# An RWKV and band-attention encoder layer: the sample streams' eight RWKV steps as a second chain beside the prompt's first sixteen

## The chip, the cores and the metric

One core of one Trainium2 chip. The time is the device time of one execution in microseconds (us), the median of several runs. Lower is better.

## What is computed

One inference step of a one-layer streaming encoder, in float32, with d_model 1024, 1024 prompt rows of one new stream and 16 rows of each of 8 running sample streams:

```python
x = x + 0.5 * SwiGLU_1(RMSNorm(x))
P = RMSNorm(x) @ w_in        # r,k,v + three loras for RWKV-7; q,k,v for attention
mix = concat(RWKV7(P_rwkv), BandAttn(P_att)) @ w_out
x = x + mix
x = x + 0.5 * SwiGLU_2(RMSNorm(x))
y = RMSNorm_final(x)

def step(s, inp):            # RWKV-7, per head: state s is 64 x 64, one row after the other
    sa = einsum('bhvk,bhk->bhv', s, kk_t)
    s = s * w_t - sa * (kk_t * a_t) + v_t * k_t
    y_t = einsum('bhvk,bhk->bhv', s, r_t)
```

The prompt begins with a zero state, each sample stream with one from the inputs (`state_wkv`), and every last state is an output. Eight heads of 64 in either group. Attention looks back over a band of eight chunks of 64.

## The kernel before, in words

The kernel runs through stages: the first feed-forward block, the projection `P` with the preparation of the RWKV factors, the projection of attention's values, the RWKV chain beside attention, the output projection, the second feed-forward block. The rows are cut into 9 tiles of 128, eight of the prompt and one of the samples. Products are made of split high and low parts of the operands, three matmuls for one.

**The RWKV chain.** Rows are taken 32 at a time (`L`): 32 prompt steps that follow one another, since each takes the state that the one before left, and 8 steps of the sample streams (one per stream, 16 rows), which take a state from the inputs and have nothing to do with each other. They are grouped by four: groups i = 0 to 7 are the prompt, 8 and 9 the streams. One step (in `_rwkv_run`, L942) is a chain from engine to engine: eight small matmuls into `ps_c` (L961, called pw below), a copy `wx` on VectorE (L963), eight matmuls (L966, pu), four copies into `mov` in turn on VectorE and ScalarE (L969), eight matmuls that make the next state (L971, wst), and two multiplications on VectorE (L984) that write the state into the next step's `mov`. Beside it eight matmuls into `ps_yc` (L975) and a copy of ScalarE (L986) give the step's output. A group's output is normalized a step at a time during the next group (`_rwkv_post`, L1014: VectorE, GpSimd, ScalarE, four transposes into `ps_y` on TensorE at L1038, and four multiplications `yo` at L1042). States come in by `_sample_states` (L929: load `sin`, four transposes into `ps_si`, a copy) and go out by `_state_out` (L1000: transposes into `ps_so`, a copy `so`, a store from SP's queue). `ps_yc`, `ps_si`, `ps_so` and `ps_y` are all one PSUM bank (`_post_bank`, L925), and `ps_c` is another.

**The order of the work.** The tile scheduler gives every engine one fixed list of instructions. It follows the order of the program, and an instruction that waits holds those behind it on its engine. The program (L1389 to L1424) writes 12 prompt steps, then `_attention_inputs` (L545), whose 432 matmuls into `ps_av` (L567 to L569) need nothing of the chain and stand between its steps on TensorE. After them the program has one group of the chain, then six units of attention, and so on. `_attention` (L1203) has 72 units (a pair of heads, a row tile, a head of the pair), 18 to each of four pairs of heads. Its loads (`q`, `kt`, `v`, `bias`) are issued on GpSimd's queue, the RWKV loads on SP's.

Of the kernel before, what the change touches and what calls it, by code (L numbers as in the profile page):

```python
# [9 lines left out]
F32 = mybir.dt.float32  # L10
# [6 lines left out]
P = 128  # L17
# [9 lines left out]
HD = 64  # L27
# [850 lines left out]
def _chunk_constants(k, a):  # L878
    nc = k.nc

    def t(shape, name):
        return k.rw.tile(shape, F32, tag=name, bufs=1, name=name)


    k.wst = [t([P, NPAIR, 2, 2, P], f"wst{i}") for i in range(2)]
    for w in k.wst:
        nc.vector.tensor_copy(w[0:HD].rearrange("r p e i (h d) -> r (p e i h) d", d=HD),
                              k.ident[0:HD, None, 0:HD].to_broadcast([HD, 4 * NH, HD]))


def _rwkv_load(k, i):
# [7 lines left out]
    rw = k.rw  # L899
# [3 lines left out]
    if j == 0:  # L903
        k.tt = rw.tile([P, 2, 8, L], F32, tag="tt", bufs=2, name="tt")
        nc.sync.dma_start(k.tt.rearrange("s a c t -> s (a c t)"), k.inv[:, :, g].rearrange("b s x t -> (b s) (x t)"))
    q.tt = k.tt[:, :, cj]
# [15 lines left out]
    return q  # L922
# [19 lines left out]
def _rwkv_run(k, a, i, pq, q, nq):  # L942

    nc = k.nc
    mm = nc.tensor.matmul
    rw = k.rw
    q.y = rw.tile([P, 4, 2, HD], F32, tag="y", bufs=2, name="y")
    post = iter(()) if pq is None else _rwkv_post(k, i - 1, pq)
    fin = None
    if i == 7:  # L950
        fin = rw.tile([HD, 1, NH, HD], F32, tag="y", bufs=2, name="fin")
    for c in range(4):
        cc = 4 * i + c
        mov, wout = q.mov[:, c], q.wout[:, :, c]
        wst = q.wst[:, :, c % 2, c // 2].rearrange("r p (h d) -> r p h d", d=HD)
        pw, pu = (k.cbank[:, 128 * j:128 * j + 128].rearrange("p (a d) -> p a d", a=2)
                  for j in (cc % 2, 1 - cc % 2))
        px = k.cbank[:, 256:].rearrange("p (a d) -> p a d", a=NPAIR)
        for hh in HEAD_ORDER:
            s = slice(L * (hh // 2), L * (hh // 2) + L)  # L960
            mm(pw[s, hh % 2], wout[0:HD + L, hh, 0:L], mov[0:HD + L, hh], start=True, stop=True)  # L961
        wx = rw.tile([P, 2, HD], F32, tag="wx", bufs=2, name="wx")
        nc.vector.tensor_copy(wx, pw)  # L963
        for hh in HEAD_ORDER:
            s = slice(L * (hh // 2), L * (hh // 2) + L)
            mm(pu[s, hh % 2], q.tt[s, hh % 2, c], wx[s, hh % 2], start=True, stop=True)  # L966
        for j in range(4):
            copy = nc.scalar.copy if j % 2 else nc.vector.tensor_copy
            copy(mov[HD + L:P, 2 * j:2 * j + 2], pu[L * j:L * j + L])  # L969
        for hh in range(NH):  # L970
            mm(px[HEADS[hh % 2], hh // 2], wst[:, hh // 2, hh % 2], mov[:, hh], start=True, stop=True)  # L971
        py = _post_bank(k, "ps_yc")[:, :P].rearrange("p (a d) -> p a d", a=2)
        for hh in HEAD_ORDER:
            s = slice(L * (hh // 2), L * (hh // 2) + L)
            mm(py[s, hh % 2], wout[:, hh, L:], mov[:, hh], start=True, stop=True)  # L975
        if i == 7 and c == 3:
            nxt = fin[:, 0]
        elif i >= 8:
            nxt = mov[0:HD]
        else:  # L980
            nxt = q.mov[0:HD, c + 1] if c < 3 else nq.mov[0:HD, 0]
        for h in range(2):
            s = HEADS[h]
            nc.vector.tensor_tensor(nxt[:, h:NH:2], px[s],  # L984
                                    k.pc[s, :, cc:cc + 1].to_broadcast([HD, NPAIR, HD]), ALU.mult)
        nc.scalar.copy(q.y[:, c], py)  # L986
        next(post, None)
        if c == 1 and 7 <= i < 2 * NG - 1:
            _sample_states(k, a, i - 7, nq.mov)
    if i == 2 * NG - 1:  # L990
        for _ in _rwkv_post(k, i, q):
            pass
    if i == 7:
        _state_out(k, fin, lambda p: k.o["wkv_p"][0, 0:1, 2 * p:2 * p + 2])
    elif i >= 8:
        b0 = 4 * (i - 8)
        _state_out(k, q.mov, lambda p: k.o["wkv_s"][0, b0:b0 + 4, 2 * p:2 * p + 2])
# [51 lines left out]


def _rwkv(k, a):
    _chunk_constants(k, a)
    k.cbank = k.psc.tile([P, 512], F32, tag="c", bufs=1, name="ps_c")
    n = 2 * NG
    pq, q = None, _rwkv_load(k, 0)
# [470 lines left out]
```

## Time and profile before

| | |
|---|---|
| median of 3 runs | 2610.01 us (2602.8 to 2616.19) |
| profiled execution, its own time | 2605.25 us |
| its span in the profile | 2603.5 us |
| TensorE busy in the span | 2422.6 us (93%) |
| VectorE, ScalarE, GpSimd busy | 1124.8, 899.8, 1076.5 us |
| value projection ends, first attention softmax, last attention output | 1367.9, 1405.0, 1660.5 us |

Times inside the kernel are read on the profiled execution from the start of its span. The granted clock is the share of full speed that TensorE got in a stretch: 1.00 is 2.4 GHz, 0.50 is 1.2 GHz, and a value between is a mixture of the two. PEld are TensorE's weight loads, and SPq, ACTq are the DMA issues of a queue's engine.

### The profile page before, as it was taken

The page shows a single profiled execution, that of the slowest core. Times are in us where ns is not written, and L with a number is a line of the kernel's source. Part 1 is how long each engine was busy: PE and PEld are TensorE (multiplying, and loading weights), DVE is VectorE, ACT ScalarE, POOL GpSimd, SP SyncE. Part 2 cuts the span into 40 slices and gives each one's busy share as a digit, 9 for nine tenths or more (in the row PEclk, how much of TensorE's full clock was granted, in tenths as well). Part 3 has the DMA queues.
Part 4 walks back from the last instruction along what each step waited for, and adds up shares of the span by engine and source line. Part 5 has one row for each costly group of instructions (what it writes and reads, how often), then busy time and mean ns, then how long its engine had stood idle before and what let it go on. Part 6 is the DMA issues. An engine that isn't in the chain of part 4 may idle for free.

```text
span 2603.5 us, 43481 instructions
## 1 busy us (share of the span) xinstructions
PE 2422.6 (93%) x17415; PEld 2161.5 (83%) x17415; DVE 1124.8 (43%) x2346; ACT 899.8 (35%) x1903; POOL 1076.5 (41%) x966
## 2 busy tenths in 40 slices
PE   4999999988999999999997999897999999989998
PEld 3899999986888799899874666676999999988886
DVE  6322222214544533856854666346222222225555
ACT  5333333321111443443323576524333333321112
POOL 4545454444433233443213443105554544544332
PEclk8999999999999999999996899998999999999999
DMA  3222112227322324543658994522221122252221
GB/s 113 67 68 86 56 63 86 67 83 269 113 77 70 107 63 133 168 132 104 190 148 197 219 206 112 175 91 65 67 86 57 62 86 68 69 197 102 77 102 73
DMA packets 230283, 284.75 MB, mean 109 GB/s; under 512 B 54920, under 2 KB 183552, under 8 KB 227264
## 3 DMA queue, kind: packets, MB, share of 16 engines
q1 hardware_dynamic: 194044, 226.72, 27.8%
q0 software_dynamic: 7648, 25.43, 4.1%
q10 hardware_dynamic: 28388, 29.81, 3.5%
q8 instruction: 137, 2.24, 0.4%
q14 instruction: 66, 0.54, 0.1%
HBM read 191.79 MB, written 90.12 MB: 108 GB/s over the span
## 4 chain that ended last, share of the span: by engine, by line
PE 42%; DVE 5%; POOL 3%; issue 3%; ACT 2%; DMA 2%; ACTq 0%; POOLq 0%; DVEq 0%
PE pa L341 3%; PE pd L450 3%; PE pd L451 3%; PE pd L449 3%; PE pa L343 3%; PE pa L342 3%; PE pb L341 2%; PE pb L342 2%; PE pb L343 2%; POOL frm L292 2%; PE ps_s L1132 1%; PE ps_o L1186 1%; PE ps_pt L1171 1%; PE ps_yc L975 1%; PE ps_wo L1261 1%
## 5 line engine op out<-in xcount | busy, mean ns | idle before, releaser
L341 PE MATMUL pa<-F,frm 128*128 128x256 f32 (+1 forms) x1408 | 424.6, 302 | 34.7 <-ACT r L348 25.2
L343 PE MATMUL pa<-F,frm 128*128 128x256 f32 (+1 forms) x1408 | 419.3, 298 | 2.7 <-POOL frm L292 2.7
L342 PE MATMUL pa<-F,frm 128*128 128x256 f32 (+1 forms) x1408 | 419.3, 298 | 2.1 <-POOL F L272 2.1
L453 DVE TENSOR_TENSOR x<-pd,x 128x512 f32<-128x512 f32 x396 | 270.0, 690 | 243.1 <-PE pd L451 228.8
L163 POOL TENSOR_TENSOR spl<-raw,spl 128x1024 fp32r<-128x1024 f32 x78 | 187.6, 2408 | 453.0 <-ACT spl L162 453.0
L449 PE MATMUL pd<-spl,h 128*128 128x512 f32 x792 | 314.0, 397 | 14.8 <-ACT spl L162 12.1
L450 PE MATMUL pd<-spl,h 128*128 128x512 f32 x792 | 311.9, 394 | 13.3 <-POOL spl L163 13.3
L292 POOL TENSOR_TENSOR frm<-cmb,frm 128x512 fp32r<-128x512 f32 x176 | 230.1, 1309 | 221.7 <-ACT frm L291 221.3
L343 PE MATMUL pb<-F,frm 128*128 128x320 f32 (+1 forms) x1056 | 312.7, 296 | 3.1 <-POOL frm L292 3.1
L342 PE MATMUL pb<-F,frm 128*128 128x320 f32 (+1 forms) x1056 | 312.2, 296 | 3.1 <-DVE F L271 3.1
L341 PE MATMUL pb<-F,frm 128*128 128x320 f32 (+1 forms) x1056 | 313.3, 297 | 1.2 <-ACT frm L291 1.2
L451 PE MATMUL pd<-spl,h 128*128 128x512 f32 x792 | 311.8, 394 | 0.0
L341 PEld LDWEIGHTS pa<-F,frm 128*128 128x128 f32 x1408 | 268.9, 191 | 44.4 <-ACT r L348 33.0
L343 PEld LDWEIGHTS pa<-F,frm 128*128 128x128 f32 x1408 | 269.1, 191 | 3.5 <-POOL frm L292 3.5
L342 PEld LDWEIGHTS pa<-F,frm 128*128 128x128 f32 x1408 | 269.4, 191 | 2.5 <-POOL F L272 2.5
L292 POOL TENSOR_TENSOR frm<-raw,frm 128x512 fp32r<-128x512 f32 x132 | 173.8, 1318 | 186.7 <-ACT frm L291 186.7
L162 ACT ACTIVATE spl<-raw 128x1024 fp32r<-128x1024 f32 x78 | 82.2, 1055 | 406.3 <-PE pd L451 342.7
L343 PEld LDWEIGHTS pb<-F,frm 128*128 128x128 f32 x1056 | 200.2, 190 | 3.8 <-POOL frm L292 3.8
L342 PEld LDWEIGHTS pb<-F,frm 128*128 128x128 f32 x1056 | 200.1, 190 | 3.3 <-DVE F L271 3.3
L341 PEld LDWEIGHTS pb<-F,frm 128*128 128x128 f32 x1056 | 200.0, 189 | 1.8 <-ACT frm L291 1.8
L449 PEld LDWEIGHTS pd<-spl,h 128*128 128x128 f32 x792 | 150.1, 190 | 48.5 <-ACT spl L162 12.3
L450 PEld LDWEIGHTS pd<-spl,h 128*128 128x128 f32 x792 | 150.1, 189 | 48.3 <-POOL spl L163 16.2
(259 smaller groups left out, 4572.7 us busy)
## 6 DMA issues: line engine op xcount, KB each, us to landing
raw<-in_w_ff_gate_dram SPq DMA_DIRECT2D x22, 1024.0 KB
raw<-in_w_ff_up_dram SPq DMA_DIRECT2D x22, 1024.0 KB
raw<-in_w_ff_down_dram SPq DMA_DIRECT2D x44, 512.0 KB
raw<-in_w_in_dram SPq DMA_DIRECT2D x26, 512.0 KB
hr<-hd SPq DMA_DIRECT2D x11, 1152.0 KB
hr<-he SPq DMA_DIRECT2D x11, 1152.0 KB
q<-qk POOLq DMA_DIRECT2D x24, 384.0 KB, 7.6
x<-xd SPq DMA_DIRECT2D x18, 512.0 KB
```

What stands on the lines that cost most here:

```text
L162: k.nc.scalar.activation(dst[:, 0], raw, AF.Copy)
L163: k.nc.gpsimd.tensor_tensor(dst[:, 1], raw, dst[:, 0].bitcast(F32), ALU.subtract)
L292: nc.gpsimd.tensor_tensor(d[:, 1], x, d[:, 0].bitcast(F32), ALU.subtract)
L341: nc.tensor.matmul(ps, frm[:, 0, c], F[:, 0, jj, c], start=new and c == 0, stop=False, **kw)
L342: nc.tensor.matmul(ps, frm[:, 0, c], F[:, 1, jj, c], start=False, stop=False, **kw)
L343: nc.tensor.matmul(ps, frm[:, 1, c], F[:, 0, jj, c], start=False, stop=c == 3, **kw)
L449: mm(ps, h[:, 0, f, a], d[f][:, 0, b], start=f == 0, stop=False)
L450: mm(ps, h[:, 0, f, a], d[f][:, 1, b], start=False, stop=False)
L451: mm(ps, h[:, 1, f, a], d[f][:, 0, b], start=False, stop=f == 1)
L453: nc.vector.tensor_tensor(xs, ps, xs, ALU.add)
L975: mm(py[s, hh % 2], wout[:, hh, L:], mov[:, hh], start=True, stop=True)
L1132: mm(ps, q.qs[i // 3][:, j, h, t:t + P], q.ks[h][:, c0:c0 + n], start=j == 0, stop=j == 1)
```

## The change

The chain is split. `_rwkv` is the prompt alone and yields after every step. `_rwkv_samples` is a second generator for groups 8 and 9, with a pool of its own (`rw2`, one buffer for each of `mov`, `wout`, `wst`, `tt` and `y`) and a PSUM bank of its own (`ps_cs`). Both issue the same step, now `_chunk`. The program writes sixteen prompt steps with a stream step after every second one from the fourth on, then the value projection, then the other sixteen prompt steps with two units of attention after each. To make room, `sin` and `so` share a tag of two buffers (before: four and two), the normalization's square shares the tag of `yo`, the factors `gb` are loaded late into one buffer (before: with a group's other loads into one of two), and the pool `iv` of the inversion is closed early. Where `rw2` lay, attention's keys `kt` come to lie, once the streams have left it.

```diff
+def _state_weights(k, rw, n):
 ...
-def _rwkv_load(k, i):
+def _rwkv_load(k, i, rw, wst, bufs):
 ...
-    q.mov = rw.tile([P, 4, NH, HD], F32, tag="mov", bufs=2, name="mov")
+    q.mov = rw.tile([P, 4, NH, HD], F32, tag="mov", bufs=bufs, name="mov")
 ...
+def _gates_load(k, i, q, rw):
 ...
-    q.gb = rw.tile([P, NPAIR, 2, n], F32, tag="gb", bufs=2, name="gb")
+    q.gb = rw.tile([P, NPAIR, 2, n], F32, tag="gb", bufs=1, name="gb")
 ...
-        sin = k.rw.tile([P, 4, HD], F32, tag="sin", bufs=4, name="sin")
+        sin = k.rw.tile([P, 4, HD], F32, tag="sin", bufs=2, name="sin")
 ...
-def _rwkv_run(k, a, i, pq, q, nq):
+def _chunk(k, bank, i, c, q, nxt):
 ...
-        so = k.rw.tile([P, 4, HD], F32, tag="so", bufs=2, name="so")
+        so = k.rw.tile([P, 4, HD], F32, tag="sin", bufs=2, name="so")
 ...
-    sq = rw.tile([P, NH, HD], F32, tag="gn_sq", bufs=1, name="gn_sq")
+    sq = rw.tile([P, NH, HD], F32, tag="yo", bufs=1, name="gn_sq")
 ...
+def _rwkv_samples(k, a, rw, psum):
+
+    bank = psum.tile([P, 512], F32, tag="cs", bufs=1, name="ps_cs")
+    wst = _state_weights(k, rw, 1)
+    for i in range(8, 2 * NG):
+        q = _rwkv_load(k, i, rw, wst, 1)
+        q.y = rw.tile([P, 4, 2, HD], F32, tag="y", bufs=1, name="y")
+        _sample_states(k, a, i - 8, q.mov)
+        for c in range(4):
+            _chunk(k, bank, i, c, q, q.mov[0:HD, c])
+            yield
+        _gates_load(k, i, q, k.rw)
+        for _ in _rwkv_post(k, i, q):
+            pass
+        b0 = 4 * (i - 8)
+        _state_out(k, q.mov, lambda p: k.o["wkv_s"][0, b0:b0 + 4, 2 * p:2 * p + 2])
 ...
         chain = _rwkv(k, a)
-        for _ in range(3):
-            next(chain)
+        next(chain)
+        s_iv.close()
+        with ExitStack() as s:
+            streams = _rwkv_samples(k, a, pool(s, "rw2"), pool(s, "psum_s", space=PSUM))
+            for n in range(1, 16):
+                next(chain)
+                if n > 1 and n % 2:
+                    next(streams)
+            for _ in streams:
+                pass
         _attention_inputs(k, a)
 ...
             for _ in chain:
-                for _ in range(6):
+                for _ in range(2):
                     next(units, None)
```

The first place is on TensorE, where the value projection ends. Of the kernel before, its last rows, where prompt step 8 (counted from 0) ends and step 9 begins; L961 is pw, L966 pu, L971 wst:

```order
L567 MATMUL ps_av<-spl,xg 128x256
L568 MATMUL ps_av<-spl,xg 128x256
L971 MATMUL ps_c<-mov,wst_12331 64x64 x8
L975 MATMUL ps_yc<-mov,wout 32x64 x5
L569 MATMUL ps_av<-spl,xg 128x256
L567 MATMUL ps_av<-spl,xg 128x256
L568 MATMUL ps_av<-spl,xg 128x256
L569 MATMUL ps_av<-spl,xg 128x256
L961 MATMUL ps_c<-mov,wout 32x64 x8
L966 MATMUL ps_c<-wx,tt 32x64 x8
```

And of the change, where the lines of a step are L955 (pw), L960 (pu), L965 (wst) and L969, and L937 is a stream state's transposes:

```order
L567 MATMUL ps_av<-spl,xg 128x256
L568 MATMUL ps_av<-spl,xg 128x256
L955 MATMUL ps_cs<-mov,wout 32x64 x3
L569 MATMUL ps_av<-spl,xg 128x256
L937 MATMUL ps_si<-ident,sin 64x128 x4
L955 MATMUL ps_cs<-mov,wout 32x64 x5
L960 MATMUL ps_cs<-wx,tt 32x64 x8
L960 MATMUL ps_c<-wx,tt 32x64 x8
L969 MATMUL ps_yc<-mov,wout 32x64 x3
L965 MATMUL ps_cs<-mov,wst_12530 64x64 x8
L969 MATMUL ps_yc<-mov,wout 32x64 x5
L965 MATMUL ps_c<-mov,wst_12333 64x64 x8
```

The prompt's step in `ps_c` is here step 4, counted from 0: its pw stands 130 matmuls of the value projection earlier, and its pu behind the first stream step's. Steps 5 to 8 have moved out of the value projection.

The second place is TensorE between the two groups of streams (L984 are the transposes of states that go out, L937 of states that come in, L1015 those of the normalization). Of the change:

```order
L965 MATMUL ps_c<-mov,wst_12332 64x64 x8
L969 MATMUL ps_yc<-mov,wout 32x64 x5
L1015 MATMUL ps_y<-ident,y 128x128 x4
L955 MATMUL ps_c<-mov,wout 32x64 x8
L1015 MATMUL ps_y<-ident,y 128x128 x4
L984 MATMUL ps_so<-ident,mov 128x64 x16
L937 MATMUL ps_si<-ident,sin 64x128 x8
L955 MATMUL ps_cs<-mov,wout 32x64 x2
L937 MATMUL ps_si<-ident,sin 64x128 x8
L955 MATMUL ps_cs<-mov,wout 32x64 x6
L960 MATMUL ps_cs<-wx,tt 32x64 x8
L960 MATMUL ps_c<-wx,tt 32x64 x8
```

Four states go out and four come in between pw and pu of prompt step 12; in the kernel before these transposes stood one by one among attention's matmuls.

The third place is GpSimd's list, which issues attention's loads. Of the kernel before (L1031 and L1032 belong to the normalization of group 1, L1044 ends it):

```order
L1031 TENSOR_TENSOR gn_s<-gn_s,mhalf 128x8
L1032 TENSOR_TENSOR y<-y,gn_s 128x512
L1081 DMA q<-qk_8741 64x4x384 x2
L1087 DMA kt<-qk_8844 64x384 x2
L1044 TENSOR_TENSOR yo<-yo,gb 128x512
```

And of the change (L1001 to L1021 are the normalization, and the `yo` of 256 columns is the streams'):

```order
L1021 TENSOR_TENSOR yo<-yo,gb 128x512
L1001 TENSOR_TENSOR y<-y,gn_m 128x512 x2
L1008 TENSOR_TENSOR gn_s<-gn_s,mhalf 128x8
L1009 TENSOR_TENSOR y<-y,gn_s 128x512
L1021 TENSOR_TENSOR yo<-yo,gb 128x256
L1008 TENSOR_TENSOR gn_s<-gn_s,mhalf 128x8
L1091 DMA q<-qk_8741 64x4x384 x2
L1097 DMA kt<-qk_8844 64x384 x4
```

The loads stand behind the normalization of the second streams' group and part of that of the prompt's group 3. On VectorE the first maximum of a softmax stands behind prompt step 20 (counted from 0) and behind `wx` of step 21. Between the end of the value projection and that row VectorE has eight stream steps, each paired with one of the prompt steps 4, 5, 7, 9, 12, 13, 15 and 16, and nine prompt steps by themselves (6, 8, 10, 11, 14, 17 to 20).

## Rows read from the trace of the kernel before

**Rows 1.** The page: busy time, share of the span and instructions of each engine, and the clock granted to it in 40 equal slices of the span, in tenths.

```profile
PE 2422.6 (93%) x17415; PEld 2161.5 (83%) x17415; DVE 1124.8 (43%) x2346; ACT 899.8 (35%) x1903; POOL 1076.5 (41%) x966
...
PEclk8999999999999999999996899998999999999999
```

**Rows 2.** Windows of the span, from and to in us: the length, busy time of each engine and its instructions, then granted clock, DMA share and GB/s. The value projection's end; two stretches between it and attention; the first and the last pair of attention heads.

```profile
1334.00:1368.00 34.00, 33.28 (x456) 25.84 (x458) 13.69 (x37) 7.14 (x23) 8.69 (x7) 1.00 0.51 130
1368.00:1373.00 5.00, 3.10 (x80) 1.94 (x80) 1.88 (x6) 1.11 (x4) 2.55 (x5) 1.00 0.95 218
1373.00:1404.00 31.00, 17.14 (x248) 12.04 (x248) 9.50 (x26) 3.75 (x13) 11.43 (x15) 0.50 0.83 186
...
1405.00:1476.00 71.00, 67.77 (x815) 44.99 (x816) 44.47 (x125) 44.01 (x115) 26.44 (x38) 0.79 0.96 212
...
1618.00:1660.00 42.00, 37.00 (x366) 27.41 (x366) 23.77 (x69) 35.70 (x96) 7.78 (x9) 0.96 0.39 111
```

**Rows 3.** The timeline of TensorE: start, length, line and tiles, then the idle time before and what ended it. The first matmuls of prompt step 4, and the last two of the value projection.

```profile
1334.31 0.43 PE L961 MATMUL ps_c<-mov,wout 96*32 96x64 f32 x16
...
1367.51 0.28 PE L568 MATMUL ps_av<-spl,xg 128*128 128x256 f32 x1
...
1367.63 0.28 PE L569 MATMUL ps_av<-spl,xg 128*128 128x256 f32 x1
```

**Rows 4.** The timeline over prompt step 9, the first after the value projection, to the first matmuls of step 10.

```profile
1367.92 0.43 PE L961 MATMUL ps_c<-mov,wout 96*32 96x64 f32 x16
...
1368.77 0.43 PE L966 MATMUL ps_c<-wx,tt 32*32 32x64 f32 x16 [0.41 <-DVE wx L963]
...
1370.62 0.69 PE L971 MATMUL ps_c<-mov,wst 128*64 128x64 f32 x16
...
1371.42 0.85 DVE L984 TENSOR_TENSOR mov<-ps_c,pc 64x256 f32<-64x256 f32 x2 [1.15 <-PE ps_c L971]
...
1372.33 0.43 PE L961 MATMUL ps_c<-mov,wout 96*32 96x64 f32 x16 [0.69 <-DVE mov L984]
```

**Rows 5.** The timeline over prompt step 11 to the first matmuls of step 12, with the transposes and the multiplications of a group's normalization.

```profile
1380.49 0.65 PE L961 MATMUL ps_c<-mov,wout 96*32 96x64 f32 x16 [0.46 <-DVE mov L984]
...
1381.56 0.65 PE L966 MATMUL ps_c<-wx,tt 32*32 32x64 f32 x16 [0.41 <-DVE wx L963]
...
1383.57 1.12 PE L971 MATMUL ps_c<-mov,wst 128*64 128x64 f32 x16
...
1384.80 0.86 DVE L984 TENSOR_TENSOR mov<-ps_c,pc 64x256 f32<-64x256 f32 x2 [1.63 <-PE ps_c L971]
...
1385.71 1.09 PE L1038 MATMUL ps_y<-ident,y 128*128 128x128 f32 x4 [0.45 <-ACT y L986]
1386.72 0.42 PEld L961 LDWEIGHTS ps_c<-mov,wout 96*32 96x32 f32 x16 [0.33 <-DVE gn_m L1022]
...
1386.89 0.89 DVE L1042 TENSOR_TENSOR yo<-ps_y,gb 128x128 f32<-128x128 f32 x4 [0.52 <-PE ps_y L1038]
```

**Rows 6.** Windows of one us each, with the columns of rows 2, where the granted clock fell and where it rose again.

```profile
1372.00:1373.00 1.00, 0.43 (x16) 0.27 (x16) 0.45 (x2) 0.00 (x0) 0.00 (x0) 1.00 1.06 241
1373.00:1374.00 1.00, 0.59 (x16) 0.35 (x16) 0.30 (x2) 0.00 (x0) 0.00 (x0) 0.64 1.29 242
...
1420.00:1421.00 1.00, 1.00 (x8) 0.64 (x6) 0.14 (x1) 1.00 (x3) 0.00 (x0) 0.50 0.94 360
1421.00:1422.00 1.00, 1.00 (x8) 0.53 (x6) 0.17 (x1) 0.53 (x3) 0.00 (x0) 0.96 0.98 360
```

**Rows 7.** The timelines of GpSimd (the first issue of attention's loads, the issue of its first bias) and of VectorE (the first addition of it, the first maximum of a softmax).

```profile
1368.01 1.49 POOL L1081 DMA_DIRECT2D q<-qk  x2
...
1393.82 0.59 POOL L1091 DMA_DIRECT2D bias<-bias  x1
...
1404.45 0.50 DVE L1142 TENSOR_TENSOR ps_s<-ps_s,bias 128x128 f32<-128x128 f32 x2 [3.94 <-DMA bias<-bias]
1404.97 0.29 DVE L1154 TENSOR_REDUCE nm<-ps_s 128x1 f32<-128x128 f32 x1
```

**Rows 8.** The timelines of VectorE (the first maximum of the second, third and fourth pair of heads, and the last one of all) and of ScalarE (the last copy of attention's output).

```profile
1475.76 0.29 DVE L1154 TENSOR_REDUCE nm<-ps_s 128x1 f32<-128x128 f32 x1
...
1548.69 0.27 DVE L1154 TENSOR_REDUCE nm<-ps_s 128x1 f32<-128x128 f32 x1
...
1617.99 0.29 DVE L1154 TENSOR_REDUCE nm<-ps_s 128x1 f32<-128x128 f32 x1
...
1655.65 0.42 DVE L1154 TENSOR_REDUCE nm<-ps_s 128x1 f32<-128x256 f32 x1
...
1660.23 0.27 ACT L1198 COPY am<-ps_o 128x128 f32<-128x128 f32 x1 [1.41 <-PE ps_o L1194]
```

**Rows 9.** States that go out and come in: the timeline of ScalarE (the copies of the prompt's last state, the third of which waits for a store), of SP's queue (the loads of a group's `wst`), and, as a group of a tile's instructions, ScalarE's copies of states that come in (least, median and longest in ns, first and last start).

```profile
1546.06 0.22 ACT L1010 ACTIVATE so<-ps_so 128x64 f32<-128x64 f32 x1 [1.36 <-PE ps_so L1007]
1546.85 0.22 ACT L1010 ACTIVATE so<-ps_so 128x64 f32<-128x64 f32 x1 [0.57 <-PE ps_so L1007]
1551.37 0.23 ACT L1010 ACTIVATE so<-ps_so 128x64 f32<-128x64 f32 x1 [0.23 <-DMA out_dram<-so]
...
1335.54 10.65 SPq L915 DMA_DIRECT2D wst<-wsd  x2
...
L938 ACT COPY mov<-ps_si x8: 569/580/581, 1529.4 to 1572.9; 64x512 f32<-64x512 f32 x8
```

More of the change, by code (lines that the diff above doesn't have):

```diff
@@ L875, in _invert @@
         nc.sync.dma_start(k.inv[p][:, g0:g1].rearrange("s g x t -> (g x) s t"), w[r])
-def _chunk_constants(k, a):
-    nc = k.nc
[L881 to L888, printed above, removed]
-def _rwkv_load(k, i):
-    nc = k.nc
-    rw = k.rw
+def _state_weights(k, rw, n):
+    ws = [rw.tile([P, NPAIR, 2, 2, P], F32, tag=f"wst{i}", bufs=1, name=f"wst{i}") for i in range(n)]
+    for w in ws:
+        k.nc.vector.tensor_copy(w[0:HD].rearrange("r p e i (h d) -> r (p e i h) d", d=HD),
+                                k.ident[0:HD, None, 0:HD].to_broadcast([HD, 4 * NH, HD]))
+    return ws
+def _rwkv_load(k, i, rw, wst, bufs):
+    nc = k.nc
     g, j = divmod(i, 2)
@@ L946, in _rwkv_run @@
     rw = k.rw
[L947 to L997, printed above, removed]
+    cc = 4 * i + c
+    mov, wout = q.mov[:, c], q.wout[:, :, c]
+    wst = q.wst[:, :, c % 2, c // 2].rearrange("r p (h d) -> r p h d", d=HD)
+    pw, pu = (bank[:, 128 * j:128 * j + 128].rearrange("p (a d) -> p a d", a=2)
+              for j in (cc % 2, 1 - cc % 2))
@@ new lines, in _chunk @@
+    px = bank[:, 256:].rearrange("p (a d) -> p a d", a=NPAIR)
+    for hh in HEAD_ORDER:
+        s = slice(L * (hh // 2), L * (hh // 2) + L)
+        mm(pw[s, hh % 2], wout[0:HD + L, hh, 0:L], mov[0:HD + L, hh], start=True, stop=True)
+    wx = rw.tile([P, 2, HD], F32, tag="wx", bufs=2, name="wx")
+    nc.vector.tensor_copy(wx, pw)
+    for hh in HEAD_ORDER:
+        s = slice(L * (hh // 2), L * (hh // 2) + L)
+        mm(pu[s, hh % 2], q.tt[s, hh % 2, c], wx[s, hh % 2], start=True, stop=True)
@@ new lines, in _chunk @@
+    for j in range(4):
+        copy = nc.scalar.copy if j % 2 else nc.vector.tensor_copy
+        copy(mov[HD + L:P, 2 * j:2 * j + 2], pu[L * j:L * j + L])
+    for hh in range(NH):
+        mm(px[HEADS[hh % 2], hh // 2], wst[:, hh // 2, hh % 2], mov[:, hh], start=True, stop=True)
+    py = _post_bank(k, "ps_yc")[:, :P].rearrange("p (a d) -> p a d", a=2)
+    for hh in HEAD_ORDER:
+        s = slice(L * (hh // 2), L * (hh // 2) + L)
+        mm(py[s, hh % 2], wout[:, hh, L:], mov[:, hh], start=True, stop=True)
@@ L1000, in _state_out @@
+    for h in range(2):
+        s = HEADS[h]
+        nc.vector.tensor_tensor(nxt[:, h:NH:2], px[s],
+                                k.pc[s, :, cc:cc + 1].to_broadcast([HD, NPAIR, HD]), ALU.mult)
+    nc.scalar.copy(q.y[:, c], py)
 def _state_out(k, st, dst):
@@ L1384, in tile_encoder_step @@
         k.pbufs = 5
-        k.iv = pool(s_xg, "iv", "right")
+        s_iv = ExitStack()
+        k.iv = pool(s_iv, "iv", "right")
         k.niv = 2
```

45 lines of the change are left out of this document (31 added, 14 removed).

## The prediction, made before the change had run

> **What bounds the kernel now.** I read the page first: TensorE is busy for 93% of the span and the clock is at full in most slices, with a dip where the RWKV chain runs [rows 1]. So the question is where TensorE idles and at which clock it runs there. The windows answer by stage [rows 2]. While the value projection lasts (1334 to 1368), TensorE is busy 33.28 of 34 us: the chain's steps lie in its gaps, and a step costs only its matmuls. From 1373 to 1404, where the chain runs by itself, TensorE is busy 17.14 of 31 us, at a granted clock of 0.50, which is 1.2 GHz. In attention it is busy again: 67.77 of 71 us in the first pair of heads.
>
> The chain by itself is bound by its own links. At 2.4 GHz a step takes from pw at 1367.92 to the next pw at 1372.33, 4.41 us [rows 4]. At 1.2 GHz it takes from 1380.49 to the end of its two multiplications, 1384.80 + 0.86, or 5.2 us [rows 5].
>
> Attention started when its first bias had landed: its issue at 1393.82 stood on GpSimd between pieces of the normalization, the addition that waited for it began at 1404.45, the first maximum at 1404.97 [rows 7]. Attention ends at 1660.23 + 0.27 = 1660.5 [rows 8], 255.5 us later. The last pair's 18 units have their first maximum at 1617.99 and their last at 1655.65 [rows 8]. By then the chain is done, so a pair without steps takes 37.66 × 18/17 = 39.9 us, and the last one 42.5 to its end. Bare attention is 3 × 39.9 + 42.5 = 162 us. The other 93.5 us are the 27 steps that lay in it (13 of 40 were done at its start): **3.4 us a step** in round numbers, in two ways close to its matmuls alone.
>
> So a step costs some 3 us where other matmuls stand around it and 4.4 to 5.2 us where none do. The change moves steps between these places.
>
> **The change, part by part.** All times are of the profiled execution: 2605.25 us, 0.2% under the median.
>
> *1. Out of the value projection: a gain now, paid later.* From step 4's pw at 1334.31 the list has 131 matmuls of the projection left, with no step between them (the first place of the order). Their spacing is 0.12 us [rows 3]: 15.7 us, and 1.5 for three groups of state transposes (four of 128 x 128 take 1.09 at 1.2 GHz [rows 5], about half at 2.4), so it ends near 1351.5, not 1367.9. But five steps that were covered are now not done.
>
> *2. The start of the streams.* Their loads are on SP's queue, where the pair of `wst` loads was held for 10.65 us in this stretch [rows 9]. Bounds: 0, if they land under the projection, and 11, if TensorE waits through a hold like it. I take 4, since half of such a hold lies under the projection. So the joint rounds begin at 1355.5.
>
> *3. The joint rounds.* Eight rounds hold a step of either chain. No row shows one. Least: the lone step, 4.4 at 2.4 GHz, 5.2 at 1.2. Most: two lone steps one after the other, 8.8 and 10.4. On TensorE the second chain's pw, pu and wst stand directly behind the first's, which adds the one's matmul time where the other waits; VectorE and ScalarE copy for both, and the two `ps_yc` share one bank, so the second waits for the copy of the first. I take the lone step + 0.3 for VectorE + the matmuls of the other step that do not fit in its waits, 0.7 at 2.4 GHz and 1.7 at 1.2 (pu and wst, 0.65 + 1.12 [rows 5]): 5.4 or 7.2.
>
> The clock decides which. It was 1.00 after the projection and fell in the us from 1373, after five us in which TensorE was busy 3.10 [rows 2, 6] and the largest idle gap in the rows of that step is 0.69 us [rows 4]; it came back only at 1421, in attention, with TensorE fully busy [rows 6]. Joint rounds have gaps at each link. I take two rounds at 5.4 and six at 7.2: 54.0 us.
> The Trainium skill, page "TensorE: Matmul & The Clock Gate", section "Why this matters for your kernels", says that long idle gaps between bursts of matmuls are what drops the clock; by it, a stage whose gaps are all short keeps 2.4 GHz and the sum is the first rival's. Here the clock fell with short gaps alone, so I go by the rows.
>
> *4. The lone rounds.* Nine prompt steps stand by themselves (6, 8, 10, 11, 14, 17 to 20): at 5.2, 46.8 us.
>
> *5. The normalizations of prompt groups 0 to 3.* With the transposes of one, step 12's pw began at 1386.72 and not at 1385.66, and the four `yo` multiplications, 0.89, follow on VectorE ahead of the next `wx` [rows 5]. With some 0.6 for the reductions that is 2.6 each, 10 us for four. Bounds 6 (the pieces fit in the chain's waits) and 14 (the streams' fall on the path too).
>
> *6. Between the stream groups.* Prompt step 12's pu now stands behind four states out and four in, and the loads of the second group into single buffers stand behind the first's last readers (second place). A pair of `so` buffers was blocked from the copy at 1546.06 to the third at 1551.37: 5.3 us a turn [rows 9]. `sin` and `so` share these two buffers, so the path is the end of a normalization (3), two turns of stores (10.6), a load and its transposes twice (two times 4.5, by a landing like that of a store), and copies at 0.58 each [rows 9] (2.3): 25 to 26. TensorE does almost nothing meanwhile. I take 26, bounds 18 (one turn lies under the last joint round) and 32 (one more hold on SP's queue).
>
> *7. The streams' end.* Attention's keys take the place of the streams' buffers, so its loads stand on GpSimd behind the second stream group's normalization (third place), and have some 11 us from there to use, as from 1393.82 to 1404.45 [rows 7]. Four lone steps, 17 to 20, cover them; I add 4 for the last states out, bounds 0 and 10. The late `gb` loads, the earlier weight loads of the output projection and their splits are on SP, ScalarE and GpSimd, beside a chain that waits on its own links: 0, and up to 4 if ScalarE's splits hold its copies.
>
> Sum: 1355.5 + 54.0 + 46.8 + 10 + 26 + 4 = **1496** for the first maximum (now 1405).
>
> *8. Attention.* 21.5 of the 32 prompt steps and all streams are then done, so 10.5 steps stay in it: 162 + 10.5 × 3.4 = 198 us, not 255.5. It ends near 1694, against 1660.5: 33 us later. The stages behind it keep their work. 2605.25 + 33 = **2638 us**. In short: 16.5 steps leave attention, five leave the projection, where they cost 3 to 3.4 each, and all are done where a step costs 5 or more or waits for loads.
>
> **The rivals.**
>
> *The clock holds (the other side).* If the joint stage stays at 2.4 GHz, because two chains leave TensorE fewer gaps than one, its rounds cost 8 × 5.4 + 9 × 4.41 = 82.9 instead of 100.8. The start waits 0, the normalizations cost 8, the stall 18, and attention's first 16 us, now at 1.2 GHz up to 1421 [rows 6], run at 2.4 GHz (about 4 less). 18 + 4 + 2 + 8 + 4 = 36 off: 2602 us, not slower. For it: more matmuls in a row; the full clock of step 9. Against it: steps 10 to 13. It decides where the granted clock after 1355 is near 1.00 on the mean. Chance 0.2.
>
> *The two chains do not overlap,* so that the streams are not beside the prompt but between its steps. Every engine has one list, and a wait in one chain holds the other: a joint round then costs up to 10.4 at 1.2 GHz, 8 × 3.2 = 25 more, 2663 us. For it: the one bank of `ps_yc`, VectorE's copies in one row. Against it: the list alternates link by link. Chance 0.12.
>
> *The loads are later than I take.* With the start at 11 and the stall at 32, 13 more, and 23 with a second held load of 10.65: 2651 to 2661 us. For it: the hold of 10.65 us in just this stretch [rows 9] and a DMA share of 0.83 to 0.95 [rows 2]. Against it: the states are small. Chance 0.13.
>
> *My forecast,* clock at 1.2 GHz, chains overlapping, one stall: 0.5, and its own bounds (start −4 and +7, stall −8 and +6, normalizations ±4, rounds −6 and +6) give 2616 to 2661. The last 0.05 is for what I have not thought of.
>
> **The numbers.** A measurement of this kernel can tell about 0.5% from no change: 13 us, so "the same" is 2597 to 2623. Faster is half of the first rival and some of the unknown: 0.12. The same is its other half and the forecast's low end: 0.24. Slower is the rest: 0.64. The range takes in the forecast, the late loads and the serial chains to 2672 with some excess of theirs, and reaches down to 2602.
>
> **What would show it.** In the profile of the changed kernel: the last matmul of the value projection near 1351; a granted clock of 0.50 in most of the stretch to the first maximum; that maximum at 1496 (1485 to 1510); one idle stretch of TensorE of some 20 us around the states' transposes; pairs of heads of 39.9 + 3.4 a step; attention's end at 1694. I am wrong in step 3 if joint rounds take under 6 or over 9 us, in step 6 if the states' turn costs under 15 us, in step 8 if attention's loads, and not the list of VectorE, set the first maximum.

## The result: 1.4% slower, and the profile after

| | before | predicted | after |
|---|---|---|---|
| median, us | 2611.86 (4 runs, 2602.80 to 2616.19) | 2638 (2602 to 2672) | 2648.32 (4 runs, 2639.43 to 2653.66) |
| ratio to before | | 1.013 on the profiled run | 1.0141, 95% interval 1.0101 to 1.0180 |
| value projection ends | 92.9 | 76.5 | 76.7 |
| first stream round begins | | 80.5 | 81.5 |
| first maximum of a softmax | 130.0 | 221 | 227.1 |
| last attention output | 385.5 | 419 | 428.1 |

The lower rows are us from the first matmul of the value projection, since the profiled run of the changed kernel (2653.66 us, span 2652.0) is the slowest of its four, and 6.3 us of its excess arose before this stage. These two rows give the zero: a line's instructions, their least, median and longest time in ns, the first and the last start. Before:

```profile
L567 PE MATMUL ps_av<-spl,xg x144: 274/283/562, 1275.0 to 1367.4; 128*128 128x256 f32 x144
```

After:

```profile
L567 PE MATMUL ps_av<-spl,xg x144: 274/283/561, 1281.3 to 1357.0; 128*128 128x256 f32 x144
```

Behind the last attention output both kernels need 943 us, so what the change did lies in this stage: 428.1 - 385.5 = 42.6 us more in these two profiles, 36.5 by the medians.

The page of the changed kernel (clock in 40 slices, against [rows 1]) shows a deeper dip in the clock, two slices at 0.5 where there was one at 0.6:

```profile
span 2652.0 us, 43489 instructions
...
PEclk9999999989999999999985588998999999999999
```

Windows of the changed kernel, columns as in [rows 2]: the wait ahead of the first stream round, the rounds of the first stream group, the gap between the two groups, the rounds of the second, and the last steps before attention.

```profile
1358.00:1363.00 5.00, 0.56 (x12) 0.29 (x11) 0.00 (x0) 0.96 (x2) 0.00 (x0) 0.94 0.42 98
...
1376.00:1408.00 32.00, 25.03 (x461) 18.05 (x460) 16.23 (x47) 10.00 (x26) 15.33 (x9) 0.61 0.70 158
1408.00:1443.00 35.00, 14.53 (x120) 9.22 (x120) 5.46 (x19) 5.89 (x13) 8.35 (x7) 0.50 0.59 135
1443.00:1472.00 29.00, 24.74 (x466) 18.27 (x468) 13.05 (x41) 5.46 (x21) 1.27 (x1) 0.56 0.19 48
1472.00:1508.00 36.00, 23.59 (x392) 17.40 (x380) 14.95 (x45) 7.29 (x24) 16.77 (x22) 0.50 0.73 162
```

Before, one stretch of 31 us ahead of attention was at 1.2 GHz with TensorE idle for almost half of it [rows 2]; now it is most of the 100 us from 1408 on and of the stretch before.

VectorE's copies `wx` (L957) are the pulse of the two chains; `ps_c` is the prompt's, `ps_cs` the streams'. Prompt steps 11 to 15, with the first stream of the second group:

```profile
1407.77 0.29 DVE L957 COPY wx<-ps_c 128x128 f32<-128x128 f32 x1 [0.77 <-PE ps_c L955]
1443.17 0.29 DVE L957 COPY wx<-ps_cs 128x128 f32<-128x128 f32 x1 [14.64 <-PE ps_cs L955]
1443.38 0.28 DVE L957 COPY wx<-ps_c 128x128 f32<-128x128 f32 x1
1450.17 0.29 DVE L957 COPY wx<-ps_c 128x128 f32<-128x128 f32 x1 [0.78 <-PE ps_c L955]
...
1456.83 0.29 DVE L957 COPY wx<-ps_c 128x128 f32<-128x128 f32 x1
1462.31 0.29 DVE L957 COPY wx<-ps_c 128x128 f32<-128x128 f32 x1 [0.78 <-PE ps_c L955]
```

Two joint rounds take 6.8 and 6.7 us, the lone step behind them 5.5, and between steps 11 and 12 lie **35.6 us**. The timeline inside that gap:

```profile
1412.27 1.09 PE L1015 MATMUL ps_y<-ident,y 128*128 128x128 f32 x4 [0.45 <-ACT y L974]
...
1422.36 1.12 PE L1015 MATMUL ps_y<-ident,y 128*128 128x128 f32 x4 [8.42 <-POOL y L1009]
...
1424.34 0.66 PE L984 MATMUL ps_so<-ident,mov 64*128 64x64 f32 x4 [0.86 <-DVE yo L1019]
...
1427.65 0.38 ACT L987 ACTIVATE so<-ps_so 128x256 f32<-128x256 f32 x1
...
1432.27 0.93 SPq L934 DMA_DIRECT2D sin<-in_state_wkv_dram  x2
...
1434.58 1.03 PE L937 MATMUL ps_si<-ident,sin 128*64 128x128 f32 x4 [5.80 <-DMA sin<-in_state_wkv_dram]
...
1442.50 0.63 PE L955 MATMUL ps_cs<-mov,wout 96*32 96x64 f32 x10 [0.32 <-ACT mov L938]
```

It reads as one chain: normalizations until 1424.3 (12 us, TensorE waits 8.42 for GpSimd), the states out until 1429, their buffers and the new states' landing until 1434.6, four rounds of transposes and copies until 1442.5. Prompt step 12, whose matmuls pw were done at 1413.9, waits through all of it, because its copy stands behind the stream's on VectorE.

The start of the first joint round, on TensorE and ScalarE:

```profile
1357.80 0.60 PE L937 MATMUL ps_si<-ident,sin 128*64 128x128 f32 x4
...
1358.79 3.38 ACTq L583 DMA_DIRECT2D out_dram<-vt  x5
1362.21 0.58 ACT L938 COPY mov<-ps_si 64x512 f32<-64x512 f32 x1 [3.82 <-DMA out_dram<-vt]
...
1362.84 0.63 PE L955 MATMUL ps_cs<-mov,wout 96*32 96x64 f32 x10 [4.44 <-ACT mov L938]
```

The states had landed; ScalarE could not copy the last of them, since it was issuing the value cache's stores. Last, GpSimd's first issue of attention's loads, the first maximum and the last output, which answer to [rows 7, 8]:

```profile
1493.15 1.49 POOL L1091 DMA_DIRECT2D q<-qk  x2
...
1508.44 0.49 DVE L1164 TENSOR_REDUCE nm<-ps_s 128x1 f32<-128x128 f32 x2
...
1709.12 0.27 ACT L1208 COPY am<-ps_o 128x128 f32<-128x128 f32 x1 [1.41 <-PE ps_o L1204]
```

### The profile page after: what moved, and what is told of

Same layout as the page of the kernel before. It is cut to its first block, busy times and chain, and to the rows that moved or that the text cites. A ratio compares the mean times of both kernels' runs of the same rounds, so it can differ in the third digit from the quotient of the medians.

```text
span 2652.0 us, 43489 instructions
## 1 busy us (share of the span) xinstructions
PE 2426.6 (92%) x17415; PEld 2175.5 (82%) x17415; DVE 1118.6 (42%) x2347; ACT 897.4 (34%) x1903; POOL 1078.2 (41%) x966
## 4 chain that ended last, share of the span: by engine, by line
PE 66%; DVE 8%; issue 7%; POOL 7%; DMA 7%; ACT 4%; ACTq 0%; POOLq 0%; SPq 0%; DVEq 0%
PE pa L341 6%; PE pd L449 6%; PE pd L451 6%; PE pd L450 6%; PE pa L343 6%; PE pa L342 6%; PE pb L341 3%; PE pb L342 3%; PE pb L343 3%; POOL frm L292 3%; PE ps_p L226 2%; PE ps_p L227 2%; PE ps_p L228 2%; DVE cmb L297 1%; PE ps_wo L1271 1%
## 5 line engine op out<-in xcount | busy, mean ns | idle before, releaser
L163 POOL TENSOR_TENSOR spl<-raw,spl 128x1024 fp32r<-128x1024 f32 x78 | 187.5, 2407 | 491.8 <-ACT spl L162 491.8
```

The source lines that it names most:

```text
L163: k.nc.gpsimd.tensor_tensor(dst[:, 1], raw, dst[:, 0].bitcast(F32), ALU.subtract)
```

## Experiments

All ran beside the kernel before; a ratio is against it. Stage times are us from the first matmul of the value projection, "end" is the last maximum of a softmax: before 130.0 and 380.7, after 227.1 and 423.3.

| run | median, us | ratio, 95% interval | first maximum | end |
|---|---|---|---|---|
| e1, late | 2648.44 | 1.0154 (1.0112 to 1.0195) | 228.7 | 427.3 |
| e2, states out first | 2642.14 | 1.0145 (1.0104 to 1.0187) | 216.7 | 414.0 |
| e3, one chain after the other | 2673.05 | 1.0257 (1.0222 to 1.0292) | 252.8 | 450.1 |
| e4, further transposes | 2651.83 | 1.0178 (1.0143 to 1.0212) | 239.4 | 431.0 |
| e5, in a bank of their own | 2641.92 | 1.0130 (1.0105 to 1.0156) | 228.5 | 420.3 |
| e6, late, loads early | 2640.65 | 1.0124 (1.0099 to 1.0150) | 224.3 | 411.8 |
| e7, out, then load | 2641.42 | 1.0126 (1.0102 to 1.0150) | 212.2 | 417.3 |
| e8, e6 and e7 together | 2625.16 | 1.0062 (1.0038 to 1.0087) | 210.3 | 396.8 |
| e9, prompt alone | 2606.43 | 0.9993 (0.9974 to 1.0012) | 126.8 | 382.7 |
| e10, in the hole | 2615.12 | 1.0026 (1.0010 to 1.0042) | 150.3 | 382.6 |

**e1: the streams three steps later.**

```diff
-                if n > 1 and n % 2:
-                    next(streams)
+                if n > 6:
+                    next(streams, None)
```

> The streams begin three prompt steps later in the program (behind prompt step 6 and then one after every step, instead of one after every second from step 2), so that prompt steps 4 to 7 and the first matmuls of step 8 stand beside the value projection again. Theory (steps left the cover because prompt step 4 stands behind the first stream step): the projection ends some 15 to 17 us later than in the changed kernel, the wait of 4 to 5 us at its end is gone, and four to five rounds of 5 to 7 us are saved behind it: first softmax maximum 6 to 12 us earlier, 2636 to 2642 us. Rival (the steps were only delayed by the streams' loads, and the cover is worth nothing): first maximum within 3 us of the changed kernel's, 2648 us.

Nothing was gained. Steps 4 to 7 ran beside the projection (6.0 to 7.2 us from copy to copy), but the first stream round began 18 us behind the projection's end. SP's queue and TensorE in this run:

```profile
1366.94 0.38 SPq L1024 DMA_DIRECT2D mix<-yo  x1
1367.37 0.58 SPq L907 DMA_DIRECT2D wout<-grd  x1
1372.57 1.24 SPq L910 DMA_DIRECT2D wst<-wsd  x2
1373.85 1.17 SPq L934 DMA_DIRECT2D sin<-in_state_wkv_dram  x2
...
1378.28 1.03 PE L937 MATMUL ps_si<-ident,sin 128*64 128x128 f32 x4 [10.24 <-DMA sin<-in_state_wkv_dram]
```

The streams' states were issued last of the streams' loads: ahead of them on the queue stood the store of a normalization (`mix`), the streams' own second `wout` right behind it, and `wst`. What `wst` waited for, these rows do not settle. So neither the theory nor the rival was tested, but a new wait found; e6 takes it away.

**e2: the states out ahead of the normalization.**

```diff
+        b0 = 4 * (i - 8)
+        _state_out(k, q.mov, lambda p: k.o["wkv_s"][0, b0:b0 + 4, 2 * p:2 * p + 2])
         _gates_load(k, i, q, k.rw)
         for _ in _rwkv_post(k, i, q):
             pass
-        b0 = 4 * (i - 8)
-        _state_out(k, q.mov, lambda p: k.o["wkv_s"][0, b0:b0 + 4, 2 * p:2 * p + 2])
```

> The streams' last states are written out ahead of the group's normalization instead of behind it; nothing else. Theory (the gap of 35.6 us between the copies wx of prompt steps 11 and 12 is one chain of normalization, states out, states in): the normalization's 12 us (from the transposes at 1412.2 to those of the states at 1424.3) leave that chain, the gap falls to 22 to 25 us, and the kernel to 2634 to 2640 us. Rival (the gap is set by the loads' queue and buffers alone): gap 33 to 36 us, 2648 us.

The gap fell to 30.3 us, less than expected. The states went out from 1408.8 to 1414.0, but the next ones were issued behind the normalization's store on SP's queue:

```profile
1419.37 0.37 SPq L1024 DMA_DIRECT2D mix<-yo  x1
...
1420.47 1.10 SPq L934 DMA_DIRECT2D sin<-in_state_wkv_dram  x2
```

The end came 9.3 us earlier; the medians alone don't separate it from the changed kernel.

**e3: the streams behind the prompt's sixteen steps.**

```diff
-                if n > 1 and n % 2:
-                    next(streams)
```

> No stream step stands among the first sixteen prompt steps: the eight stream steps follow them one by one, with the same pools and banks. Theory (the chains overlap: a joint round takes 7.2 us and a lone one 5.2): eight lone stream steps cost 8 x 5.2 = 42 us where the joint rounds cost 8 x 2.0 = 16, so 26 more; the prompt steps 4 to 8 are covered again, about 12 less, and the wait at the start is hidden, 4 less: some 10 us slower than the changed kernel, 2652 to 2664 us. Rival (the chains do not overlap, they only hold each other): 12 to 16 us faster than the changed kernel, 2632 to 2637 us.

The end is 26.8 us later than after the change: eight lone stream steps, 5.6 us each at 1.2 GHz, do not overlap anything. The copies `wx` of prompt step 15 and of the first two streams:

```profile
1403.95 0.29 DVE L957 COPY wx<-ps_c 128x128 f32<-128x128 f32 x1 [0.77 <-PE ps_c L955]
...
1425.72 0.29 DVE L957 COPY wx<-ps_cs 128x128 f32<-128x128 f32 x1 [15.21 <-PE ps_cs L955]
...
1431.31 0.29 DVE L957 COPY wx<-ps_cs 128x128 f32<-128x128 f32 x1 [0.78 <-PE ps_cs L955]
```

A plain joint round costs 1.2 to 1.6 us over a lone step at the same clock, so the chains do overlap. I had expected some 10 us and not 27. The cover came back: the copy of prompt step 9 stood at 92.8 us from the stage's zero, after the change at 114.3. The other 16 us are a wait that I had not reckoned: the first streams' states were late again, and 21.8 us lie between the first two copies above, where a lone step takes 5.6. Without that wait, by an estimate (26.8 - 16.2), the run would still be some 10 us later than the changed kernel, and the rival wanted it 12 to 16 us faster: it is out.

**e4: eight transposes a step that nothing reads.**

```diff
+    lone = i >= 8 or 4 <= cc <= 20
+    rest = bank[:, 128 * (1 - cc % 2):128 * (1 - cc % 2) + 128]
+    for _ in range(3 if lone else 0):
+        nc.tensor.transpose(rest, k.ident, k.ident)
     wx = rw.tile([P, 2, HD], F32, tag="wx", bufs=2, name="wx")
 ...
+    for _ in range(5 if lone else 0):
+        nc.tensor.transpose(rest, k.ident, k.ident)
     for h in range(2):
```

> Eight further 128 x 128 transposes of the identity in each step of the joint stage (three behind pw, five behind the step's output), into the half of the bank that is free there; nothing reads them. They take about 0.14 us each at 2.4 GHz and 0.27 at 1.2, and stand mostly in TensorE's waits. Theory (the lower clock costs some 1.5 us a joint and 0.7 us a lone round, because TensorE idles between the links): the granted clock is near 1.00 in the rounds, joint rounds take 5.5 to 6.5 us and lone ones 4.5 to 5: 10 to 16 us faster, 2632 to 2638 us. Rival (the clock matters little, the copies on VectorE and ScalarE set the rounds): rounds of 7 us and more at a clock of 1.00, and the transposes cost 5 to 15 us, 2653 to 2663 us.

The clock rose to 1.00 in most of the rounds, as expected, and they still took 5.8 us and more: copies that read the same bank waited for the transposes. Window 1400 to 1414, and the timeline inside it (L978 are the multiplications that write the state):

```profile
1400.00:1414.00 14.00, 10.54 (x232) 7.41 (x224) 6.72 (x20) 2.27 (x9) 3.74 (x3) 1.00 0.82 159
```

```profile
1410.64 0.77 PE L975 MATMUL ps_c<-ident 128*128 128x128 f32 x5
...
1411.51 0.86 DVE L978 TENSOR_TENSOR mov<-ps_c,pc 64x256 f32<-64x256 f32 x2 [2.17 <-PE ps_c L975]
```

It shows that work in the waits raises the clock, not what the clock costs.

**e5: the same in a bank of its own.** The target is `k.spare`, a bank of the streams' pool, for prompt steps 4 to 15 and the streams; the projection's pool gives one of its five banks for it.

> The same eight further transposes a step (streams and prompt steps 4 to 15), now into a PSUM bank that nothing else uses, so that no copy waits for them; the value projection has four banks instead of five for that. In the run before, the copies of the same bank waited for the transposes (a lone round took 5.8 us at 2.4 GHz). Theory (the lower clock costs 1.5 us a joint round and 0.7 a lone one): granted clock near 1.00 in the rounds, joint rounds 5.4 to 6.2 us, lone ones 4.4 to 5.0, the first softmax maximum 8 to 14 us earlier than in the changed kernel, 2634 to 2641 us. Rival (the rounds are set by the copies and waits between engines at either clock): joint rounds of 6.8 us or more, 2646 to 2656 us.

The edit did not do what was meant. The transposes into the spare bank wait for nothing, and all 160 ran beside the value projection, none in a round (here the 100 behind the outputs; the 60 behind pw ran from 1286.7 to 1307.0):

```profile
L974 PE MATMUL ps_sp<-ident x100: 272/273/330, 1287.1 to 1308.3; 128*128 128x128 f32 x100
```

The projection reached to 119 us (77 after the change); how much of that is the transposes and how much the missing bank was not tried apart. Its matmuls stood among the rounds of the first group; there the clock was 1.00, and joint rounds took 5.0 to 7.2 us with TensorE almost full. In the second group it was 0.67, and joint rounds took 7.0 and 7.1:

```profile
1380.00:1400.00 20.00, 18.00 (x344) 13.38 (x334) 12.20 (x34) 5.35 (x19) 5.02 (x4) 1.00 0.74 167
...
1440.00:1460.00 20.00, 15.93 (x326) 11.58 (x325) 9.09 (x28) 7.60 (x22) 8.12 (x4) 0.67 0.23 71
```

The first maximum came as late as after the change. The run says nothing of the clock's price; what a joint round costs at 2.4 GHz is read in e8 and e10 instead.

**e6: e1 with the first streams' loads where the change has them.** The generator yields once behind `_sample_states` of group 8, and is called at n = 2 and from n = 7 on.

> As the run in which the streams began three steps later, but the loads of the first group of streams and the transposes of its states stay where the changed kernel has them in the program (behind step 2). In that run the streams' states were issued on SP's queue only at 1373.9, behind the prompt's loads that waited for their buffers, and the first stream round came 18 us behind the projection's end. Theory (cover is worth what I reckoned, and the queue took it back): the first joint round begins 1 to 4 us behind the projection's end, the first maximum is 10 to 15 us earlier than in the changed kernel, 2633 to 2640 us. Rival (the covered steps gain nothing, whatever the loads do): 2644 to 2652 us.

The wait of 18 us is gone, and the median fell by 8 us to the edge of what was expected. But only 2.8 us of that stand ahead of the first maximum: the first stream step took 11.0 us from copy to copy, the projection's last matmuls and a normalization in it, and the three rounds behind it took 8.5, 9.7 and 7.4 us at a clock of 0.50. The first of these has pieces of a normalization, the second a wait of TensorE of 1.88 us for which the profile names nothing, and the third is plain. Attention itself was 8.7 us shorter (187.5 us from the first maximum to the last); why, I can't say from these profiles.

**e7: states out, next loads and states in, then the normalization.**

```diff
+    def load(i):
 ...
+    q = load(8)
     for i in range(8, 2 * NG):
 ...
+        b0 = 4 * (i - 8)
+        _state_out(k, q.mov, lambda p: k.o["wkv_s"][0, b0:b0 + 4, 2 * p:2 * p + 2])
+        nq = load(i + 1) if i + 1 < 2 * NG else None
         _gates_load(k, i, q, k.rw)
         for _ in _rwkv_post(k, i, q):
             pass
 ...
+        q = nq
```

> The streams' last states go out ahead of the normalization, and the second group's loads and states come in ahead of it as well. In the run that moved only the states out, SP's queue held the states to come in behind the normalization's store, from 1414.9 to 1420.5. Theory (the gap is a chain through SP's queue, and the normalization is its longest link): the gap between the copies wx of prompt steps 11 and 12 falls from 30.3 us in that run to 22 to 26, first maximum 14 to 19 us earlier than in the changed kernel, 2629 to 2636 us. Rival (the two buffers of states and the landings set the gap): gap of 29 us or more, 2640 to 2646 us.

The gap is 27.0 us: 8.6 less than after the change and 3.3 less than in e2, which is 1 us over the range of theory and 2 under the rival's. The first maximum came 14.9 us earlier, as expected, the end only 6.0, and the median 7 us lower, where the rival had it. One prompt step fewer was done by then (21 copies `wx` ahead of it, not 22), which is some 3.5 us; the rest of the difference lies in attention and is left open. What is left of the gap is states out (1410 to 1415.7), the landing of the new ones, and their transposes:

```profile
1416.74 1.36 SPq L934 DMA_DIRECT2D sin<-in_state_wkv_dram  x2
...
1421.12 1.03 PE L937 MATMUL ps_si<-ident,sin 128*64 128x128 f32 x4 [5.90 <-DMA sin<-in_state_wkv_dram]
```

**e8: e6 and e7 in one kernel.**

> Both edits: streams behind prompt step 6, first loads early, states out and in ahead of the normalization. If the two costs are separate they add: first maximum 25 to 33 us earlier than in the changed kernel, 2616 to 2625 us. Theory (a joint round of 7 us is two steps of 3.5 us, which is what a step costs in attention, so even without waits the second chain gains nothing there): still 0.3 to 0.6% slower than the kernel before. Rival (with the waits gone the second chain pays): 2605 us or less.

2625.16 us: with both waits shortened the loss falls to 0.6%, and does not vanish. The first maximum came 16.8 us earlier and not 25 to 33, with two prompt steps fewer done (20 copies `wx` ahead of it). The two edits give more together (26.5 us at the end) than one by one (11.5 and 6.0). In this run a part of the second group's rounds ran at 2.4 GHz. Windows over two rounds, and the prompt's copies at their ends:

```profile
1430.60:1436.20 5.60, 4.46 (x128) 3.22 (x128) 4.28 (x13) 1.56 (x7) 2.68 (x2) 1.00 0.50 185
1436.20:1443.00 6.80, 4.72 (x128) 3.42 (x128) 3.46 (x11) 3.67 (x8) 4.67 (x2) 1.00 0.24 80
```

```profile
1430.60 0.29 DVE L957 COPY wx<-ps_c 128x128 f32<-128x128 f32 x1
...
1436.19 0.29 DVE L957 COPY wx<-ps_c 128x128 f32<-128x128 f32 x1
```

The first has little of a normalization in it (GpSimd 2.68 us) and takes 5.6 us at 2.4 GHz; the second, with more of it, takes 6.8. A plain round of this order took 7.4 us in this run at 0.50 (copies at 1389.36 and 1396.73).

**e9: the prompt's steps moved, the streams left at the chain's end.**

> One part alone: sixteen prompt steps are written ahead of the value projection, a step with two units of attention after it, the buffers shared as in the change; but the streams come last, in the prompt's chain and pools, as in the kernel before. On VectorE the first softmax maximum stands behind 15 prompt steps (before: 14). Theory (the loss comes from the streams' second chain, which delays attention's loads): within 0.4% of the kernel before, 2600 to 2618 us, first maximum 130 to 140 us after the projection's first matmul (before 130.0, changed kernel 227.1). Rival (the moved prompt steps are to blame, since lone steps cost 5.2 us): first maximum at 160 us or later, 2620 us or more.

The same time as before, within 0.3%: the reordered prompt steps cost nothing, since the scheduler fits them in where they fitted before. As before, and not one more as expected, 14 copies `wx` stand ahead of the first maximum, which came 3.2 us sooner. Its first maximum:

```profile
1407.42 0.28 DVE L1159 TENSOR_REDUCE nm<-ps_s 128x1 f32<-128x128 f32 x1
```

**So the whole loss comes with the streams' second chain**, the prompt steps that it pushes out of the value projection included.

**e10: a second chain only where time is lost anyway.** Group 8 beside prompt steps 8 to 11, group 9 at the prompt chain's end; `ck`, `cv` and `kc` allocated ahead of `kt`.

```diff
-            for n in range(1, 16):
+            for n in range(1, 12):
                 next(chain)
-                if n > 1 and n % 2:
+                if n == 2 or n > 7:
                     next(streams)
```

> The second chain only where the kernel before waits anyway: the first four streams beside prompt steps 8 to 11, with their loads early and their states out ahead of their normalization; the other four at the end of the prompt's chain; attention's caches and keys of the samples, not its first keys, lie where the streams' buffers were. Before, 37 us between the projection's end and the first maximum held 4 to 5 lone steps. Theory (a joint round of 5.6 to 7.2 us is two steps at the price that a step has in attention, so the second chain pays only in time that is lost anyway): first maximum at 140 to 155 us, with 18 steps done in place of 13, and the kernel within 0.4% of the kernel before, 2598 to 2620 us, and 1% below the changed kernel. Rival (a second chain beside the first pays in itself): 2595 us or less. Other rival (any second chain delays attention by more than it saves): 2625 us or more.

As the theory has it: first maximum at 150.3, end 1.9 us behind before's, 0.26% slower. 20.3 us of delay bought four stream steps and two prompt steps more ahead of attention, at the 3.4 to 3.5 us that a step costs there some 21 us: even. GpSimd's first load was issued only at 1407.2, behind the streams' normalization, with no shared place for the first keys any more:

```profile
1407.23 0.84 POOL L1103 DMA_DIRECT2D q<-qk  x1
```

This run also shows the clock's price in one kernel. Windows over two joint rounds that follow each other, with the same matmuls and nothing on GpSimd:

```profile
1378.20:1385.60 7.40, 6.82 (x129) 5.08 (x130) 3.44 (x11) 1.55 (x6) 0.00 (x0) 0.53 0.55 120
1385.60:1391.00 5.40, 4.31 (x128) 3.18 (x128) 3.40 (x11) 1.55 (x6) 0.00 (x0) 1.00 0.18 50
```

They take 7.4 us at 1.2 GHz and 5.4 at 2.4: the clock is worth some 2 us a round. In e1 two plain rounds took 5.1 us each at 1.00 (the prompt's copies at 1452.53, 1457.66 and 1462.80).

No version beat the kernel before.

## Why the prediction was right

**Step 1** (five steps out of the cover): the projection ended at 76.7 us, predicted 76.5. That it is a loss later is shown only in part: e1 and e6 put the steps back, and other waits took most of it.

**Step 2** (4 us at the streams' start): 4.44 us, but by another cause, so the size was luck. I named SP's queue; the states had landed, and ScalarE was held by its issues of the value cache's stores. SP's hold is real where the streams begin later (e1).

**Step 3** (joint rounds): the eight rounds, read between the prompt's copies `wx`, are 57.5 us, predicted 54.0, the longest (9.25, 7.3, 7.2) with pieces of a normalization in them; plain ones take 6.7 to 6.8 at 1.2 GHz, in the order of e6, e8 and e10 7.4 (predicted 7.2), and at 2.4 GHz 5.1 (e1) and 5.4 (e10; predicted 5.4). That the chains overlap is shown by e3. The granted clock was 0.50 to 0.61 in most of the stage, as the rows of before had it.
The Trainium skill, page "TensorE: Matmul & The Clock Gate", section "Why this matters for your kernels", has long idle gaps between bursts of matmuls as what drops the clock. The trace agrees for one fall and disagrees for another. The clock was 0.50 from 1363 on, right behind the idle of 4.44 us at the streams' start. It rose in the us from 1369, and fell again in the us from 1372 with no idle of TensorE over 0.41 us since 1367.6:

```profile
1370.63 0.43 PE L960 MATMUL ps_c<-wx,tt 32*32 32x64 f32 x16 [0.41 <-DVE wx L957]
...
1371.00:1372.00 1.00, 0.72 (x24) 0.39 (x13) 0.78 (x4) 0.48 (x2) 0.00 (x0) 1.00 1.22 206
...
1373.00:1374.00 1.00, 1.00 (x20) 0.71 (x19) 0.57 (x2) 0.10 (x1) 0.00 (x0) 0.50 1.13 370
```

**Steps 4 and 5** (lone rounds, normalizations): eight lone steps took 49.7 us between copies; 8 x 5.2 + 10 = 51.6 was reckoned.

**Step 6** (between the groups): 35.6 - 5.2 = 30.4 us, predicted 26, bounds 18 and 32. The size was near, its parts were not: I took 3 us for the normalization and 10.6 for two turns of stores, and that the errors partly cancel is luck. The normalizations took 12, and the states out 5, without waiting for a buffer (the third copy at 1427.65 follows the second by 1.45 us; before it was 4.5 [rows 9]). e2 and e7 took 5.3 and 8.6 us out of the gap by moving the normalization behind. It is the mis-sized term: normalization 12, not 3, of which those edits gave back only part, since the loads and landings behind it stayed.

**Step 7** (the end): 15.3 us from GpSimd's first issue to the first maximum, covered by steps 19 and 20 as reckoned; VectorE's own list set it, with step 21's copies just ahead.

**Step 8** (attention): 201.0 us against 198. The prediction counted 13 steps as done when attention began before; 14 copies `wx` stand ahead of it, and of the 14th step only its last two multiplications were left:

```profile
1405.18 0.84 DVE L984 TENSOR_TENSOR mov<-ps_c,pc 64x256 f32<-64x256 f32 x2
```

So 15.5 steps left attention and not 16.5. From before's 255.5 that is 54.5 us less: 3.5 each, reckoned 3.4. In the forecast the miscount nearly cancels, since the price was taken from the same 255.5 us.

The sum was 9.6 us short in the profiled run and 3.5 in the medians, of which the gap is 4.4. The first rival (the clock holds) fell with the windows, the second (no overlap) with e3. The third (late loads, 2651 to 2661) was near the truth in time and not in cause: what brought the gap near its upper bound was the normalization.

Put as one account: attention began 97.1 us later, with 15.5 more steps done. That is 6.3 us for each, and in attention each had cost 3.5. Two chains side by side at 1.2 GHz bring a step down to 3.4 us (6.8 a round of two), which is only what attention asks for it. At 2.4 GHz it would be 2.6 to 2.7 (e1, e10), which is less, but no run held that clock through the stage. The waits around the streams (4.4 and 30.4) and the lone steps between are the loss.

**What stays open:** why attention was shorter in e6 and e8 than after the change, and why the clock came back for whole rounds in e1, e8 and e10, and only for parts of rounds after the change.

## What to carry to other kernels

Before moving a latency-bound chain out of a stage, price a step where it is and where it goes: beside a full TensorE it costs its matmuls, by itself its links, and overlapping two such chains may only bring it back to the first price. A second chain brings its own loads, stores and single buffers; in engines with one fixed list its waits hold the first chain too, so count the instructions of the first that stand behind each of them. Test the reordering and the second chain apart: one kernel (e9) told which of the two cost the time.

## What the runs showed of the hardware

Much the same joint rounds ran at a granted clock of 0.56 after the change, with TensorE busy 24.74 of 29 us, and at 1.00 in e8, with 4.46 of 5.6, and in e10 at 0.53 and 1.00 one behind the other (7.4 and 5.4 us); I had taken the level for settled by the rounds themselves. Eight transposes a step that nobody reads brought 1.00 in most rounds where they stood in them (e4), but copies from the bank that they write waited for them: the state's multiplications began 1.83 us after the state's matmuls (1409.68 to 1411.51), where at the same clock it was 0.80 [rows 4].
